# Six layer norms finished block by block inside the last products, the router likewise, and expert tokens split in the order of their columns

## The chip, the core and the metric

The kernel runs on one core of one Trainium2 chip. The metric is the device time of one execution in microseconds (us), from its first to its last instruction with what lies around them. TensorE (PE) multiplies a stationary operand, which a separate load instruction brings into the array, with a moving operand; VectorE (DVE), ScalarE (ACT) and GpSimd (POOL) do the rest, and SyncE (SP) issues nearly all DMAs. Before: 2105.73 us, the median of 3 runs (2105.18 to 2108.71).

## What is computed

A first network of two layers on 256 tokens of 1024 columns, each layer three steps with a layer norm behind each, and then a second block with a gated mixer and a mixture of 32 experts:

```python
for l in range(DEPTH):                      # DEPTH = 2
    x = _layernorm(ALPHA * x + 0.5 * _swiglu(x, ffn1_w_in[l], ffn1_w_out[l]), ln1_g[l], ln1_b[l])
    mix = _hybrid_mixer(x, l, ...)
    x = _layernorm(ALPHA * x + mix, ln2_g[l], ln2_b[l])
    x = _layernorm(ALPHA * x + 0.5 * _swiglu(x, ffn2_w_in[l], ffn2_w_out[l]), ln3_g[l], ln3_b[l])
...
h = modulate(rms_norm(x, norm_mix), shift1, scale1)
x = x + gate1[:, None, :] * mixed           # mixed from h
h2 = modulate(rms_norm(x, norm_ffn), shift2, scale2)
x = x + gate2[:, None, :] * hierarchical_moe(h2, ...)   # top 2 of 8 experts in the top group of 4
```

## The kernel before

The 256 tokens are two blocks of 128 rows (`tb` 0 and 1). Every fp32 matrix product is made of three with operands split into a rounded part and its remainder (`hi`, `lo` of weights; `xh`, `xl`, `hh`, `hl` of activations): `split` (L303) casts on ACT and subtracts on DVE. Weights come tile by tile: `wload` (L278) has a DMA of 512 KB on SP into one of 4 `raw` buffers, then a split into 5 `hi` and 5 `lo` buffers. `execute` (L257) walks the list of weight tiles and has the loads run two tiles ahead.

The kernel is written against a framework that puts each engine's instructions into an order of its own: by the order in which they are written, by what is ready in its model of time, and by priority (`high_priority(n)` moves instructions ahead by n; `keep_in_program_order` fixes one where it is written). Buffers are taken from pools (`big`: 14 tiles of 128x2048). Each engine then works strictly in its order.

**The end of each step.** `outp` (L440) makes the output product. For each of its `kt` weight tiles (22 after an FFN, 8 after a mixer) it issues, for both token blocks, six products of 512 columns (two column halves, three products each). The last four tiles are held: all their 24 products for block 0 come first, then `fn(0)`, then the 24 for block 1, then `fn(1)`. `fn` is the closure of `finisher` (L478): residual and statistics (L500, L501), mean and variance (L503), reciprocal root with a power on POOL (L313, L314), gain and bias (L508, L509). In `fn(1)` first block 0's x is turned by `to_T` (L519): eight PE transposes (L331) of 128x128 into PSUM, then `split` into `xhl`, the stationary or moving operand of the next step; at its end block 1's x likewise. In the last of the six norms (`mod=True`) `fn` also calls `modnorm` (L1256): squares on ACT, mean and power, then on DVE two passes with gain (L1275) and shift (L1277) held as rows for all partitions (`gain1`, two DMAs that copy a row to 128 partitions).

**The start of each step.** `tok` with `lead=True` (L349; mixer and second block) or `lead` in `ffn` (L545) collect its four weight tiles and then issue block 0's products (24, or 48 of half the columns) and block 1's. Tiles 1 and 2 (tile 1 in the second block) are split into `s2` buffers early (`SPARE`, `SPARE2`).

**The router.** `gated` (L1829) makes the same for the second block: `head` scales the router's weights and makes 16 small instructions for constant logits during the mixer; `fn(tb)` adds the gated result to x (L1859, L1860), squares (L1264), turns x (L1869), makes logits of 36 columns (L1873) and calls `tokens` (L1928): ACT writes rms-scaled tokens (L1933), DVE their remainder (L1935), both in a permuted order, column q*8+k to place k*128+q. `moe` (L2250) adds x to the output by eight products with the identity (L2257), `route` (L1938) is a chain of some 40 small DVE instructions to a one-hot table and places. `batch` (L2212) then builds selection matrices `P` (L2220) and gathers the tokens of four experts with PE (L2245): stationary 128 columns of the token tiles (tile name `raw`), moving `P`; 8 batches x 8 column groups x 4 products are 256. The experts' products are L2085 and L2122, the scatter L2141. `turn` (L2097) has the only stationary operand with a step between columns: L2107 reads every second column of `hs`, beside L2103, which reads contiguous `Pw`.

Of the kernel before, what the change touches and what calls it, by code (L numbers as in the profile page):

```python
# [18 lines left out]
NB = 2  # L19
# [12 lines left out]
PRIO = {'narrow': 300, 'rope2': 300}  # L32

SPARE, SPARE2 = (1, 2), (1,)

SUBY = (3, 9, 13)
TWO_PI = 2.0 * math.pi
# [69 lines left out]
class Net:  # L107
    def __init__(self, ctx, tc, I):
# [18 lines left out]
        self.side = None  # L127

# [149 lines left out]
    def wload(self, src, a, b, spare=False):  # L278
# [6 lines left out]
        if spare:  # L285
# [7 lines left out]
        self.split(hi[:, :n], lo[:, :n], raw[:, :n])  # L293
# [9 lines left out]
    def split(self, hi, lo, src):  # L303
        self.nc.scalar.copy(hi, src)  # L304
        self.nc.vector.tensor_tensor(lo, src, hi.bitcast(F32), op=ALU.subtract)  # L305
# [22 lines left out]
    def transposes(self, src, n=4):  # L328
        pt = self.bank([128, n, 128])
        for k in range(n):  # L330
            self.nc.tensor.transpose(pt[:, k, :], src[:, k * 128:(k + 1) * 128], self.ident)  # L331
# [3 lines left out]
    def mm_tok(self, ys, tb, ah, al, wh, wl, start, stop, parts=(0, 1)):  # L335
        mm = self.nc.tensor.matmul
        t = slice(tb * 128, tb * 128 + 128)
        for i in parts:
            for j, y in enumerate(ys):
                c = slice(j * 512, min(j * 512 + 512, wh.shape[1]))  # L340
# [8 lines left out]
    def tok(self, xT, w, c0, fn, n=512, lead=False, spare=SPARE):  # L349
# [10 lines left out]
        def tile(j):  # L360
            def run(wh, wl):
# [16 lines left out]
        for j in range(parts):  # L378
            self.W(w[:, kn * j:kn * j + kn, c0:c0 + n], kn, n, tile(j), lead and j in spare)
# [60 lines left out]
    def outp(self, aT, w, kt, fn, last=4, pre=None, order=None, join={}, pre_at=None, tail=None):  # L440
# [3 lines left out]
        def one(k, wt, tb, parts=(0, 1)):  # L444
            ah, al = aT(order[k])
            self.mm_tok(st["ys"][tb], tb, ah, al, wt[0][:, 0, :], wt[1][:, 0, :], k == 0, k == kt - 1, parts)

        def tile(k):
            def run(wh, wl):
# [12 lines left out]
                if k == kt - 1:  # L462
                    for tb in range(NB):
                        for part in ((0,), (1,)):
                            for i, wt in enumerate(st["w"]):
                                one(kt - last + i, wt, tb, part)
                        fn(tb, st["ys"][tb])
            return run

        for k in range(kt):  # L470
# [4 lines left out]
            self.W(w[:, order[k]:order[k] + 1, :], 1, D, tile(k))  # L475


    def finisher(self, S_, g, b, mod=False):  # L478
# [3 lines left out]
        def pre():  # L482
# [5 lines left out]
            if mod:  # L488
                st["m"] = self.modrows(0, 1, "gain1")
                st["h"] = self.t8([128, NB, D], F32, "h1")  # L490

        def fn(tb, ys):
            x = S_["x"][:, tb, :]
            src = st["h"] if mod else st["x"]
            if tb == NB - 1:
                self.to_T(S_, src, 0)
# [19 lines left out]
        return pre, fn  # L516


    def to_T(self, S_, x, tb):  # L519
# [3 lines left out]
        for j in range(2):  # L523
            pt = self.transposes(x[:, tb, j * 512:(j + 1) * 512])
            o = (slice(None), slice(4 * j, 4 * j + 4), slice(tb * 128, tb * 128 + 128))
            self.split(xh[o], xl[o], pt)
        if tb == NB - 1:
            S_["xT"] = (xh, xl)


    def ffn(self, S_, w_in, w_out, g, b, mod=False, first=False, side=None):
# [13 lines left out]
        def lead():  # L545
# [11 lines left out]
            def tile(j):  # L557
                def run(wh, wl):
# [9 lines left out]
                    for tb in range(NB):  # L568
                        ps = st["ps"][tb]
                        if not first:  # L570
                            for i in range(4):
                                one(i, tb)
                        sg = self.sc([128, 256], F32, "sg", True)
                        nc.scalar.activation(sg, ps[:, 0:256], AF.Silu)
# [13 lines left out]
            for j in range(4):  # L588
                c0 = (j // 2) * D_FF
                self.W(win[:, 4 * (j % 2):4 * (j % 2) + 4, c0:c0 + 256], 4, 256, tile(j), not first and j in SPARE)  # L590
# [25 lines left out]
        for f in range(1, KF // 2):  # L616
            pair(f)
            if f == 1 + first and side is not None:
                self.side = (side, 18, 4 * (KF // 2 - 2 - first) + KF - 4, 0)
        pre, fn = self.finisher(S_, g, b, mod)  # L620
        self.outp(lambda k: (H[k // 8][0][:, k % 8, :], H[k // 8][1][:, k % 8, :]), wout, KF, fn, pre=pre)
# [53 lines left out]
    def mixer(self, S_, l, L):  # L675
# [110 lines left out]
        pre, fn = self.finisher(S_, I["ln2_g"][l], I["ln2_b"][l])  # L786
        self.outp(lambda k: (L["m"][0][:, k, :], L["m"][1][:, k, :]), wo, KD, fn, pre=pre)
# [468 lines left out]
    def modnorm(self, x, G, out):  # L1256
        self.modnorm2(x, G, out, self.modnorm1(x))

    def modnorm1(self, x):
        nc = self.nc  # L1260
        ss = self.small.tile([128, 2], F32, name="ssm", tag="ssm")
        t = [self.sc([128, 512], F32, "mn") for _ in range(2)]
# [6 lines left out]

    def modnorm2(self, x, G, out, st):  # L1270
        nc = self.nc
        ss, t = st
        for n in range(2):
            c = slice(n * 512, n * 512 + 512)
            nc.vector.scalar_tensor_tensor(t[n], x[:, c], ss[:, 0:1], G[:, 1, c], op0=ALU.mult, op1=ALU.mult)  # L1275
            o, i0, i1 = out(n, t[n], G[:, 0, c])
            nc.vector.tensor_tensor(o, i0, i1, op=ALU.add)  # L1277

    def block2(self, S_, us):
# [42 lines left out]
        for it in BLOCK2.split():  # L1322
# [14 lines left out]
            else:  # L1337
# [4 lines left out]
        self.DO(lambda: (B.update(pj=True), B["head"]()))  # L1342
        wo = I["w_out_2"][0].rearrange("(k p) n -> p k n", p=128)
        pre, fn, B["head"] = self.gated(S_, B)
        self.outp(lambda k: [a[:, k % 4, :] for a in B["m", k // 4]], wo, KD, fn, pre=pre, order=(4, 5, 6, 7, 0, 1, 2, 3),
                  join={4: "gdn"}, pre_at=4, tail=lambda: us[1]["gu"]())
# [482 lines left out]
    def gated(self, S_, B):  # L1829
# [9 lines left out]
        def head():  # L1839

            t = self.hi_p.tile([128, 1024], F32, name="hi", tag="hi")
            wr, B["wr"] = (t[:, i * 288:i * 288 + 288].rearrange("p (k n) -> p k n", k=KD) for i in range(2))
            nc.sync.dma_start(wr[:, :, 0:4], I["w_group_2"][0].rearrange("(k p) n -> p k n", k=KD))
            nc.sync.dma_start(wr[:, :, 4:36], I["w_router_2"][0].rearrange("(k p) n -> p k n", k=KD))
            nc.vector.tensor_tensor(B["wr"], wr, self.modc[:, 32:40].rearrange("p (k o) -> p k o", o=1).to_broadcast([128, KD, 36]), op=ALU.mult)
            ps = self.bank([128, 36], pj=True)
            for k in range(KD):
                nc.tensor.matmul(ps, self.modc[:, 24 + k:25 + k].to_broadcast([128, 128]), wr[:, k, :], start=k == 0, stop=k == KD - 1)
            B["lc"] = self.route_p.tile([128, 36], F32, name="lc")
            nc.vector.tensor_tensor(B["lc"][:, 0:4], ps[:, 0:4], self.v2["b_group_2"], op=ALU.add)  # L1850
            nc.vector.tensor_tensor(B["lc"][:, 4:36], ps[:, 4:36], self.v2["b_router_2"], op=ALU.add)
            B["rs"], B["t"], B["lo"] = [], [], []

        def fn(tb, ys):
# [6 lines left out]
            if tb == 0:  # L1861
                B["pr"] = self.bank([128, 2, 36], pj=True)
            nrm = self.modnorm1(x)
            B["rs"].append(nrm[0][:, 0:1])
            hT = []
            for j in range(2):
                pt = self.bank([128, 4, 128], pj=True)
# [573 lines left out]
```

## Time and profile before

| | |
|---|---|
| median of 3 runs | 2105.73 us (2105.18 to 2108.71) |
| profiled execution, its time / its span | 2107.98 / 2106.2 us |
| PE busy | 2057.2 us, 98% |
| DVE, ACT, POOL busy | 70%, 52%, 4% |
| mean granted TensorE clock | 0.990 |
| DMA | 427.6 MB, mean 203 GB/s |

Busy is the time in which an engine executes, as a share of the span from first to last instruction. An idle time is put down to what released the engine, most often a semaphore of another engine's instruction. A line as L331 can be that of a helper that several callers use; the tile names tell them apart. Product ends are modelled, so 24 products that follow each other have a pace (start to start) that is shorter than the duration of one.

### The profile page before, as it was taken

How to read it: one execution, taken by the hardware profiler on the slowest of the kernel's cores; microseconds unless marked ns; L12 is line 12 of the kernel's file. 1: busy time of each engine (PE TensorE's matmuls, PEld its weight loads, DVE VectorE, ACT ScalarE, POOL GpSimd, SP SyncE). 2: the span in 40 equal slices, each digit the busy share in tenths (PEclk: the TensorE clock that was granted, in tenths of full speed). 3: DMA queues.
4: the chain of work that ended last, by engine and by line, in shares of the span. 5: the costliest groups of instructions: out<-in, count | busy, mean ns of one | idle time of the engine just before them, and what ended most of it. 6: DMA issues, size and time to landing. Idle time of an engine off the chain costs nothing.

```text
span 2106.2 us, 30863 instructions
## 1 busy us (share of the span) xinstructions
PE 2057.2 (98%) x11507; PEld 1650.7 (78%) x11507; DVE 1470.6 (70%) x2782; ACT 1105.4 (52%) x2026; POOL 75.3 (4%) x64
## 2 busy tenths in 40 slices
PE   8999999999999999999999999999998999899998
PEld 7887877888888888888877888888887878645543
DVE  6886688987878677875688896877666675533333
ACT  5654565777655544554466776754553554322222
POOL 0000000100000000000000110000000121001000
PEclk9999999999999999999999999999999989999999
DMA  7985544454659676876544355565674423799996
GB/s 229 304 261 175 166 133 135 129 162 141 192 193 303 190 256 197 273 242 205 162 123 142 109 161 169 151 224 167 188 235 137 136 63 116 265 364 357 357 374 235
DMA packets 278825, 427.60 MB, mean 203 GB/s; under 512 B 21806, under 2 KB 206352, under 8 KB 277648
## 3 DMA queue, kind: packets, MB, share of 16 engines
q1 hardware_dynamic: 278240, 422.44, 61.6%
q0 software_dynamic: 432, 3.15, 0.4%
q8 instruction: 92, 1.51, 0.3%
q14 instruction: 61, 0.50, 0.1%
HBM read 424.46 MB, written 1.07 MB: 202 GB/s over the span
## 4 chain that ended last, share of the span: by engine, by line
PE 86%; DVE 8%; ACT 2%; issue 1%; POOL 1%; DMA 0%; SPq 0%; ACTq 0%; POOLq 0%; DVEq 0%
PE ps L408 27%; PE ps L411 14%; PE ps L2085 6%; PE y L342 5%; PE y L343 5%; PE y L345 4%; PE ps L2122 3%; PE ps L342 3%; PE ps L345 3%; PE ps L343 3%; DVE lo L305 2%; PE ps L2245 2%; PE y L2141 1%; PE y L331 1%; PE ps L301 1%
## 5 line engine op out<-in xcount | busy, mean ns | idle before, releaser
L305 DVE TENSOR_TENSOR lo<-raw,hi 128x1024 fp32r<-128x1024 f32 (+1 forms) x556 | 660.2, 1196 | 250.5 <-ACT hi L304 175.0
L304 ACT CAST hi<-raw 128x1024 fp32r<-128x1024 f32 (+1 forms) x556 | 556.6, 1028 | 337.5 <-PE y L345 169.6
L408 PE MATMUL ps<-xhl,hi 128*128 128x512 f32 x2240 | 568.4, 395 | 0.8 <-DVE kc L181 0.8
L408 PEld LDWEIGHTS ps<-xhl,hi 128*128 128x128 f32 x2240 | 402.1, 189 | 76.2 <-issue 3.3
L411 PEld LDWEIGHTS ps<-xhl,lo 128*128 128x128 f32 x2240 | 306.1, 190 | 21.7
L411 PE MATMUL ps<-xhl,lo 128*128 128x256 f32 x2240 | 314.7, 283 | 0.0
L342 PE MATMUL y<-hi,hh 128*128 128x512 f32 x352 | 137.3, 390 | 0.0
L343 PE MATMUL y<-lo,hh 128*128 128x512 f32 x352 | 137.0, 389 | 0.0
L342 PE MATMUL ps<-hi,xhl 128*128 128x512 f32 (+1 forms) x304 | 121.8, 402 | 3.5 <-DVE ra L803 2.2
L2085 PE MATMUL ps<-wgu,hi 128*64 128x512 f32 x512 | 121.1, 594 | 0.0
L345 PE MATMUL ps<-hi,xhl 128*128 128x512 f32 (+1 forms) x304 | 118.7, 393 | 1.9 <-DVE xhl L305 1.9
L343 PE MATMUL ps<-lo,xhl 128*128 128x512 f32 (+1 forms) x304 | 120.1, 395 | 0.0
L179 ACT ACTIVATE ysum<-ps 128x256 f32<-128x256 f32 x168 | 64.3, 383 | 77.4 <-PE ps L411 73.4
L345 PE MATMUL y<-hi,hl 128*128 128x512 f32 x352 | 104.5, 389 | 0.0
L2085 PEld LDWEIGHTS ps<-wgu,hi 128*64 128x64 f32 x512 | 42.6, 137 | 68.2 <-issue 64.7
L181 DVE TENSOR_TENSOR ysum<-ysum,ps 128x256 f32<-128x256 f32 x168 | 69.3, 415 | 29.0 <-ACT ysum L179 28.7
L342 PEld LDWEIGHTS y<-hi,hh 128*128 128x128 f32 x352 | 66.1, 188 | 14.8 <-issue 1.2
L345 PEld LDWEIGHTS y<-hi,hl 128*128 128x128 f32 x352 | 66.1, 188 | 13.7
L343 PEld LDWEIGHTS y<-lo,hh 128*128 128x128 f32 x352 | 66.1, 188 | 13.5
L342 PEld LDWEIGHTS ps<-hi,xhl 128*128 128x128 f32 x304 | 58.2, 192 | 19.4 <-ACT qs L795 3.0
L179 ACT ACTIVATE sg<-ps 128x256 f32<-128x256 f32 x80 | 30.4, 380 | 80.5 <-PE ps L411 80.4
L345 PEld LDWEIGHTS ps<-hi,xhl 128*128 128x128 f32 x304 | 58.1, 191 | 15.8 <-DVE xhl L305 4.3
(604 smaller groups left out, 3192.8 us busy)
## 6 DMA issues: line engine op xcount, KB each, us to landing
raw<-in_w_mix_in_dram SPq DMA_DIRECT2D x184, 512.0 KB
raw<-in_ffn_w_in_dram SPq DMA_DIRECT2D x176, 512.0 KB
raw<-in_ffn_w_out_dram SPq DMA_DIRECT2D x88, 512.0 KB
wgu<-in_w_gate_dram SPq DMA_DIRECT2D x64, 512.0 KB
wgu<-in_w_up_dram SPq DMA_DIRECT2D x64, 512.0 KB
lo<-in_w_down_dram SPq DMA_DIRECT2D x54, 512.0 KB
wada<-in_w_ada_dram SPq DMA_DIRECT2D x96, 256.0 KB
raw<-in_w_branch_dram SPq DMA_DIRECT2D x48, 512.0 KB
```

The source lines that it names most:

```text
L179: self.nc.scalar.activation(out, pb, AF.Copy, scale=scale)
L181: self.nc.vector.tensor_tensor(out, out, pa, op=ALU.add)
L304: self.nc.scalar.copy(hi, src)
L305: self.nc.vector.tensor_tensor(lo, src, hi.bitcast(F32), op=ALU.subtract)
L342: mm(y, ah[:, t], wh[:, c], start=start, stop=False)
L343: mm(y, ah[:, t], wl[:, c], start=False, stop=False)
L345: mm(y, al[:, t], wh[:, c], start=False, stop=stop)
L408: mm(ps.rearrange("p (a b) -> p a b", a=2), h[:, k % 4, c], xh.both(k), start=k == 0, stop=False)
L411: mm(ps[:, 0:256], l[:, k % 4, c], xh[:, k, :], start=False, stop=k == KD - 1)
L2085: mm(gu[64 * e:64 * e + 64, c], u["x"](k)[:, 64 * e:64 * e + 64], w, start=k == 0 and i == 0, stop=k == KD - 1 and i == len(ws[0]) - 1)
L2122: mm = lambda *a, **kw: self.placed(pin, self.nc.tensor.matmul(*a, **kw))
L2245: nc.tensor.matmul(ps[:, j, :], B["t"][tb][i][:, 128 * k:128 * k + 128], P[:, tb, :], start=n == 0, stop=n == 3)
```

## The change

1. **Plain and modulated norms.** `outp` holds 6 tiles (8 before the second block) in place of 4 after FFNs and mixers of the first network; the first 2 (4) of them lie in `big` tiles. Block 1's products go by column halves. Before the last 6 (8) products of the second half, `mid` turns block 0 (fixed order). `fn` gets a priority of 300. Block 1 is turned by `late`, which the next step's lead calls between its products for block 0 and for block 1; in `ffn`'s lead both activations come behind both blocks' products, the first one fixed. The lead's fourth tile is split early too, and loads for early splits run up to four tiles ahead.
2. **The modulated norm.** `fn` only scales rows (half on ACT, half on DVE); gain and shift are applied after the turn, where columns lie on partitions: four instructions on ACT for the first half, four on DVE for the second, into a tile that is then split. The row copies go. `late` here also runs the constant logits of `head`, whose two loads are issued with the norm's.
3. **The router.** `outp` for the second block calls `mid` after 12 of the 16 steps of block 1: block 0's eight turns. `fn(1)` interleaves turns and logits; the split of block 0's tokens, and of block 1's, has a fixed place.
4. **Token order.** `tokens` writes rows unpermuted; `gather` reads every eighth column as its stationary operand, and the extra unit permutes when it copies from PSUM.

```diff
-SPARE, SPARE2 = (1, 2), (1,)
+SPARE, SPARE2 = {1: "s2", 2: "s2", 3: "big"}, {1: "s2", 2: "s2", 3: "own"}
+TAIL, TAIL_BIG, MID = (6, 8), (2, 4), (18, 24)
...
-                while nxt < len(ws) and len(loaded) <= ahead:
+                while nxt < len(ws) and len(loaded) <= (4 if ws[nxt][5] else ahead):
...
                 if lead:
                     if j == parts - 1:
                         for tb in range(NB):
+                            if tb == NB - 1:
+                                self.late()
                             for i, wt in enumerate(st["w"]):
                                 one(i, *wt, tb)
...
                     for tb in range(NB):
-                        for part in ((0,), (1,)):
-                            for i, wt in enumerate(st["w"]):
-                                one(kt - last + i, wt, tb, part)
-                        fn(tb, st["ys"][tb])
+                        halves = [(0,), (1,)] if mid is not None and tb == NB - 1 else [(0, 1)]
+                        for n, (c, part, i) in enumerate((c, p, i) for c in halves for p in (0, 1) for i in range(last)):
+                            if len(halves) > 1 and n == mid[0]:
+                                mid[1]()
+                            one(kt - last + i, st["w"][i], tb, (part,), c, len(halves) > 1 and last == 4 and n >= mid[0])
+                        with self.tc.high_priority(prio) if prio else ExitStack():
+                            fn(tb, st["ys"][tb])
...
             if mod:
-                h = st["h"][:, tb, :]
-                self.modnorm(st["x"][:, tb, :], st["m"], lambda n, t, s: (h[:, n * 512:n * 512 + 512], t, s))
+                x, h = st["x"][:, tb, :], st["h"][:, tb, :]
+                r = self.modnorm1(x, [h[:, 0:512], h[:, 512:1024]])[0][:, 0:1]
+                nc.scalar.activation(h[:, 0:512], x[:, 0:512], AF.Identity, scale=r)
+                nc.vector.tensor_scalar(h[:, 512:1024], x[:, 512:1024], r, None, op0=ALU.mult)
             if tb == NB - 1:
                 S_["x"] = st["x"]
-                self.to_T(S_, src, 1)
+                self.late, self.pin = late, True
+        def mid():
+            with self.tc.high_priority(PRIO["norm"]):
+                self.to_T(S_, st["h"] if mod else st["x"], 0, mod)
+        def late():
+            self.pin = False
+            if mod:
+                next(self.B["head"])
+            with self.tc.high_priority(PRIO["norm"]):
+                self.to_T(S_, st["h"] if mod else st["x"], 1, mod)
...
+            if mod:
+                y = self.sc([128, 4, 128], F32, "modx", True)
+                for k in range(4):
+                    shift, gain = (self.modc[:, i + 4 * j + k:i + 4 * j + k + 1] for i in (0, 8))
+                    if j:
+                        self.nc.vector.tensor_scalar(y[:, k, :], pt[:, k, :], gain, shift, op0=ALU.mult, op1=ALU.add)
+                    else:
+                        self.nc.scalar.activation(y[:, k, :], pt[:, k, :], AF.Identity, scale=gain, bias=shift)
+                pt = y
             self.split(xh[o], xl[o], pt)
...
-        to = lambda a: a.rearrange("p (k q) -> p q k", k=KD)
-        xv = x.rearrange("p (q k) -> p q k", k=KD)
-        nc.scalar.activation(to(th), xv, AF.Identity, scale=r)
+        nc.scalar.activation(th, x, AF.Identity, scale=r)
         B["t"].append((th, tl))
-        B["lo"].append(lambda: nc.vector.scalar_tensor_tensor(to(tl), xv, r, to(th).bitcast(F32), op0=ALU.mult, op1=ALU.subtract))
+        B["lo"].append(lambda: self.tc.keep_in_program_order(
+            nc.vector.scalar_tensor_tensor(tl, x, r, th.bitcast(F32), op0=ALU.mult, op1=ALU.subtract)))
...
-                    nc.tensor.matmul(ps[:, j, :], B["t"][tb][i][:, 128 * k:128 * k + 128], P[:, tb, :], start=n == 0, stop=n == 3)
+                    nc.tensor.matmul(ps[:, j, :], B["t"][tb][i][:, k:D:KD], P[:, tb, :], start=n == 0, stop=n == 3)
```

The calls of `outp` and the router's `fn` in the changed kernel:

```diff
-        self.outp(lambda k: (H[k // 8][0][:, k % 8, :], H[k // 8][1][:, k % 8, :]), wout, KF, fn, pre=pre)
+        self.outp(lambda k: (H[k // 8][0][:, k % 8, :], H[k // 8][1][:, k % 8, :]), wout, KF, fn, last=TAIL[mod], pre=pre,
+                  big=TAIL_BIG[mod], mid=(MID[mod], mid), prio=PRIO["norm"])
...
+            turned(1, 0)
+            logits(0, 0)
+            logits(0, 1)
+            turned(1, 1)
+            logits(1, 0)
+            logits(1, 1)
+            B["lo"][0]()
+            nrm = self.modnorm1(x)
```

## Rows read from the trace of the kernel before

**Rows 1.** The page's engines: busy us, share of the span, instructions.
```profile
PE 2057.2 (98%) x11507; PEld 1650.7 (78%) x11507; DVE 1470.6 (70%) x2782; ACT 1105.4 (52%) x2026; POOL 75.3 (4%) x64
```
**Rows 2.** Who waited, PE: line, releaser, us in total, times, longest.
```profile
PE y L331 <- DVE h L1277: 5.3, 2, 4.6
...
PE y L331 <- DVE x L509: 2.9, 5, 0.8
...
PE ps L1869 <- DVE x L1860: 2.7, 1, 2.7
PE ps L301 <- DVE xhl L305: 2.4, 6, 0.6
...
PE ps L345 <- DVE xhl L305: 1.9, 3, 1.2
...
PE ps L299 <- ACT xhl L304: 1.1, 3, 0.4
...
PE ps L342 <- ACT xhl L304: 0.7, 2, 0.3
```
**Rows 3.** Timeline of PE behind two norms: start, us, instruction [idle <-releaser].
```profile
200.38 1.04 PE L331 MATMUL y<-ctab,x 128*128 128x128 f32 x8
...
211.03 0.50 PE L345 MATMUL ps<-hi,xhl 128*128 128x512 f32 x1 [0.33 <-DVE xhl L305]
...
635.99 0.39 PE L301 MATMUL ps<-hi,xhl 128*128 128x256 f32 x1 [0.56 <-DVE xhl L305]
```
**Rows 4.** Timeline of DVE, first norm, block 0.
```profile
194.90 1.28 DVE L500 SCALAR_TENSOR_TENSOR x<-x,y 128x512 f32<-128x512 f32 x2 [1.88 <-PE y L345]
...
199.05 1.41 DVE L509 SCALAR_TENSOR_TENSOR x<-x,rs,lngb 128x512 f32<-128x512 f32 x2
```
**Rows 5.** Timeline of DVE, modulated norm, block 0: its first and last instruction.
```profile
1613.27 1.29 DVE L500 SCALAR_TENSOR_TENSOR x<-x,y 128x512 f32<-128x512 f32 x2 [2.90 <-PE y L345]
...
1622.76 1.29 DVE L1277 TENSOR_TENSOR h<-mn,gain 128x512 f32<-128x512 f32 x2
```
**Rows 6.** Stretch behind it: us, busy (instructions) of PE, PEld, DVE, ACT, POOL; clock; DMA.
```profile
1621.80:1632.04 10.24, 7.34 (x20) 5.53 (x21) 10.24 (x24) 2.67 (x7) 0.92 (x1) 0.50 0.21 54
```
**Rows 7.** Timeline of PE, router: logits of both blocks, first gather.
```profile
1819.84 1.98 PE L1873 MATMUL ps<-hi,xT 128*128 128x36 f32 x16 [0.29 <-ACT xT L1871]
...
1826.11 3.63 PE L1873 MATMUL ps<-hi,xT 128*128 128x36 f32 x16
...
1836.79 0.47 PE L2245 MATMUL ps<-P,raw 128*128 128x256 f32 x2 [0.90 <-DVE P L2220]
```
**Rows 8.** Timeline of DVE, router: the split of block 1's tokens.
```profile
1830.56 1.97 DVE L1935 SCALAR_TENSOR_TENSOR raw<-x,ssm,raw 128x1024 fp32r<-128x1024 f32 x1
```
**Rows 9.** Timeline of ACT: a contiguous cast, and the permuted tokens.
```profile
1617.58 1.05 ACT L304 CAST hi<-raw 128x1024 fp32r<-128x1024 f32 x1 [8.46 <-PE y L345]
...
1826.64 2.05 ACT L1933 ACTIVATE raw<-x,ssm 128x1024 fp32r<-128x1024 f32 x1
```
**Rows 10.** Stretches of the router and of the experts, columns as in rows 6.
```profile
1823.19:1833.43 10.24, 8.40 (x25) 5.97 (x26) 5.60 (x21) 3.94 (x6) 0.56 (x1) 0.50 0.84 340
...
1836.79:2096.00 259.21, 258.89 (x1278) 127.61 (x1280) 93.24 (x207) 57.67 (x136) 8.93 (x6) 1.00 0.90 344
```
**Rows 11.** Timeline of stationary loads (PEld): turns of `Pw`, of `hs`, the gather.
```profile
1994.86 0.20 PEld L2103 LDWEIGHTS y<-ctab,Pw 128*128 128x128 f32 x2 [0.81 <-issue]
1995.03 0.31 PEld L2107 LDWEIGHTS y<-ctab,hs 128*128 128x128 f32 x2
1995.26 1.96 PEld L2245 LDWEIGHTS ps<-P,raw 128*128 128x128 f32 x16
```
**Rows 12.** Lines L2245 and L2107 by themselves: min/median/max ns, first and last start us, forms.
```profile
L2245 PEld LDWEIGHTS ps<-P,raw x256: 186/188/201, 1836.8 to 2057.3; 128*128 128x128 f32 x128
L2245 PE MATMUL ps<-P,raw x256: 276/279/392, 1836.8 to 2057.4; 128*128 128x256 f32 x128
...
L2107 PEld LDWEIGHTS y<-ctab,hs x34: 195/200/220, 1857.7 to 2090.0; 128*128 128x128 f32 x32, 64*128 64x128 f32 x2
```

More of the change, by code (lines that the diff above doesn't have):

```diff
@@ L284, in wload @@
             self.nc.sync.dma_start(rv[:, :, c], s)
-        if spare:
+        if spare == "big":
+            t = self.big.tile([128, 2048], F32R, name="wtail", tag="b8")
+            hi, lo = (t[:, i * 1024:i * 1024 + 1024] for i in range(2))
+            self.split(hi, lo, raw)
+            return (hi.rearrange("p (a b) -> p a b", a=a), lo.rearrange("p (a b) -> p a b", a=a))
+        if spare == "s2":
             hi, lo = ([self.s2.tile([128, 512], F32R, name=i, tag="sc") for _ in range(2)] for i in ("hi", "lo"))
@@ L378, in tok @@
         for j in range(parts):
-            self.W(w[:, kn * j:kn * j + kn, c0:c0 + n], kn, n, tile(j), lead and j in spare)
+            self.W(w[:, kn * j:kn * j + kn, c0:c0 + n], kn, n, tile(j), lead and spare.get(j))
     def fm(self, xT, w, c0, fn, wide=True):
@@ L474, in outp @@
                 self.JOIN(join[k])
-            self.W(w[:, order[k]:order[k] + 1, :], 1, D, tile(k))
+            self.W(w[:, order[k]:order[k] + 1, :], 1, D, tile(k), "big" if 0 <= k - (kt - last) < big else None)
     def finisher(self, S_, g, b, mod=False):
@@ L568, in run @@
                     for tb in range(NB):
-                        ps = st["ps"][tb]
                         if not first:
+                            if tb == NB - 1:
+                                self.late()
                             for i in range(4):
                                 one(i, tb)
+                    for tb in range(NB):
+                        ps = st["ps"][tb]
                         sg = self.sc([128, 256], F32, "sg", True)
-                        nc.scalar.activation(sg, ps[:, 0:256], AF.Silu)
+                        a = nc.scalar.activation(sg, ps[:, 0:256], AF.Silu)
+                        if tb == 0 and not first:
+                            self.tc.keep_in_program_order(a)
                         nc.vector.scalar_tensor_tensor(sg, sg, 0.5, ps[:, 256:512], op0=ALU.mult, op1=ALU.mult)
@@ L589, in lead @@
                 c0 = (j // 2) * D_FF
-                self.W(win[:, 4 * (j % 2):4 * (j % 2) + 4, c0:c0 + 256], 4, 256, tile(j), not first and j in SPARE)
+                self.W(win[:, 4 * (j % 2):4 * (j % 2) + 4, c0:c0 + 256], 4, 256, tile(j), not first and SPARE.get(j))
         def pair(f):
@@ L1253, in modrows, with modnorm1 @@
         return t
-    def modnorm(self, x, G, out):
-        self.modnorm2(x, G, out, self.modnorm1(x))
-    def modnorm1(self, x):
+    def modnorm1(self, x, t=None):
         nc = self.nc
         ss = self.small.tile([128, 2], F32, name="ssm", tag="ssm")
-        t = [self.sc([128, 512], F32, "mn") for _ in range(2)]
+        t = t or [self.sc([128, 512], F32, "mn") for _ in range(2)]
         for n in range(2):
@@ L1837, in pre, with turned, logits, mid @@
                 nc.sync.dma_start(B["SG"][:, i, :], self.mod[24 + 8 * i:32 + 8 * i, :].rearrange("(o f) p -> o (f p)", o=1).rearrange("o (p k) -> (o p) k", k=KD))
[L1839 to L1852, printed above, removed]
+        hT = {}
+        def turned(tb, j, pin=False):
+            pt = self.bank([128, 4, 128], pj=True)
+            for k in range(4):
+                t = nc.tensor.transpose(pt[:, k, :], S_["x"][:, tb, (4 * j + k) * 128:(4 * j + k + 1) * 128], self.ident)
+                if pin:
+                    self.tc.keep_in_program_order(t)
+            hT[tb, j] = self.sc([128, 4, 128], F32, "xT2")
+            nc.scalar.copy(hT[tb, j], pt)
+        def logits(tb, j):
+            for k in range(4 * j, 4 * j + 4):
+                nc.tensor.matmul(B["pr"][:, tb, :], hT[tb, j][:, k % 4, :], B["wr"][:, k, :], start=k == 0, stop=k == KD - 1)
+        def mid():
+            B["pr"] = self.bank([128, 2, 36], pj=True)
+            for j in range(2):
+                turned(0, j, True)
         def fn(tb, ys):
```

103 lines of the change are left out of this document (55 added, 48 removed).

## The prediction

> **What bounds the kernel now.** I read the page's engine table first: TensorE (PE) is busy 98% of the span, DVE 70%, so what moves the end is PE's idle time, its clock, or the length of its own instructions [rows 1]. Next the list of who waited for whom, for PE alone: the largest entries are turns (transposes, L331) and first products behind a layer norm, and the turn at the router [rows 2]. Then the stretches themselves: PE at the end of a plain norm [rows 3], DVE there [rows 4], DVE at the last norm, the modulated one [rows 5], the clock behind it [rows 6], the router on PE and DVE and ACT's passes [rows 7 to 9], and clock and load of router and experts [rows 10]. From the router on PE is busy 258.9 of 259.2 us, with DMA at 0.90 beside it: an experts' stage in which anything that makes a PE instruction longer lengthens the program. Last, single loads of stationary operands, because the change alters how one family of 256 of them reads SBUF [rows 11, 12].
>
> **Part A, the five plain norms.** Before, block 0's turns follow all of block 1's products, and PE waits at four places: block 1's x before its turns (2.9 us in all five), ACT's first half xhl (1.1 and 0.7), DVE's xhl (2.4 at L301; 1.9 at L345, of which 1.2 belongs to the modulated norm) [rows 2]. That is 7.8 us. The wait that follows block 1's turns, 0.33 us before a mixer and 0.56 before an FFN [rows 3], stays, since `late` still puts turns directly ahead of the products that need them: 2 x 0.33 + 3 x 0.56 = 2.3. So 5.5 us can go. Is each cover there? A product takes 0.228 us (24 of them fill about 194.90 to 200.38 [rows 3, 4]). With six held tiles PE runs 30 of block 1's 36 products, 6.8 us, before block 0's turns; that block's norm needs 194.90 to 200.46, 5.6 us [rows 4]. Six products, 1.4 us, then cover the split. Block 1's first columns end 5 us earlier than its last, so half of its x and statistics are done by then and its norm ends some 4.7 us behind the last product, under block 0's 5.5 us of next products. What is late next is a weight split standing in DVE's order ahead of the norm: 1.2 us each. I take -5.0, with bounds +1 and -7.8. The held tiles and early lead loads cost nothing beside this: the same DMAs and splits come earlier on SP, ACT and DVE, whose slack is there; without it a split of about 2.3 us (ACT then DVE) would show. Two broadcast DMAs (`gain1`) leave SP's queue; POOL keeps one power per norm.
>
> **Part B, the modulated norm.** [...] After: block 0's chain is 1613.27 to 1624.05, 10.8 us, less the two gain and shift passes on DVE (2.6) plus one scaling (0.7): about 8.5 [rows 5]; PE has 40 of 48 products before the turns, 9.1 us. Block 1's chain ends about 8 us after the last product, and PE fills 5.5 us with products and 2.0 with the 16 instructions of `head` (their like take 1.98 [rows 7]), so about 0.5 us of wait. Then the turned block must be scaled and shifted (four small instructions on ACT, four on DVE) before it is split; PE waits about 1.7 us there. That leaves 2.2 to 3 us of wait with little dense work between, so the clock may fall again, for less work than before. I take -5.0: 4 from waits, 1 from the clock; bounds -1 and -9.
>
> **Part C, the router.** Block 0's logits start at 1819.84 and the experts' first product at 1836.79; inside lie the wait of 2.7 for x behind a DVE pass that took its place, block 1's logits at the low clock (3.63 us against 1.98) and DVE's routing chain from 1829.74, with a split of tokens of 1.97 inside [rows 2, 7, 8, 10]. After: block 0's eight turns (1 us) move ahead of the last products; then turns and two blocks of logits, 5 us at the full level or about 7 if it falls again; routing without its split, 5.1; the split of block 1's tokens, now pinned behind the slot tables, about 1.4 (two contiguous halves of such a DVE pass take 1.41 [rows 4]), and the first experts' products wait for it. Together 12.5 to 14.5 instead of 18.3 from the last product on, less the moved 1 us: 3 to 5. The eight identity products of L2257 lie beside routing; if the clock is low they can end last. I take -5.0, the upper end, as ACT's pass over the tokens halves as well; bounds -1 and -8.
>
> **Part D, the gather's stationary operand.** `tokens` now writes rows as they stand, and `gather` reads every eighth column: 256 loads with a step of 32 bytes [rows 12]. No strided load of such a kind stands in the trace, so bounds from the nearest rows. Low end, no cost: the gather's loads follow each other every (1.96 - 0.19) / 15 = 0.118 us [rows 11, 12], and the one strided load there is, `turn`'s at L2107 with a step of two elements, still follows its neighbour after 0.31 - 0.20 = 0.11 us [rows 11, 12]. High end, a doubling: that same pair of loads takes 0.31 us where the contiguous pair of L2103 beside it takes 0.20 [rows 11], and ACT writing one element per 512 bytes takes 2.05 us for what it does contiguously in 1.05 [rows 9]. The logits of 36 columns, where the loads alone set the pace, take 1.98 us for 16, (1.98 - 0.28) / 15 = 0.113 each [rows 7, 12]; doubled, 0.22. 256 x (0.22 - 0.118) = 26 us, all on PE's path, as PE never idles there [rows 10]; I take +25 for a first load now and then hidden under the products before it. I choose the high end because two engines in the trace lose half their rate as soon as neighbours in the pattern are not neighbours in memory. A gain has no reason here: contiguous is already the best pattern.
>
> [...]
>
> **The sum.** -5 - 5 - 5 + 25 = +10 us. The profiled execution took 2107.98 us (span 2106.2), 2.25 above the median 2105.73 of the runs; it would become 2118, the median 2116. Own range of this case: 2108 to 2123 from gains of 8 to 23.
>
> **Rivals.** First, on the other side: strided loads keep the pace of 0.118, part D is nothing, and 2105.7 - 15 = 2091 (2082 to 2098). For it: `turn`'s loads at step two just meet that pace. Against: the halved rates. It decides at 15 / 256 = 0.06 us per load: below a spacing of 0.18 the change is a gain. Second, between: loads get slower but only by about half, to 0.16; 256 x 0.045 = 11.5, so 2102. Third: the gather as forecast, but in-order queues eat the gains: pinned turns of block 0 wait because a weight split stands before the norm on DVE, 1.2 us at each of five norms and twice at the modulated one, and PE's clock falls at both late places; gains of 3 are left, 2128. Fourth: the compiled order hardly changes, since priorities only advise it; norms gain nothing, about 2125.
>
> **How the numbers follow.** Forecast 0.44, first rival 0.38, second 0.08, third 0.07, fourth 0.03. A measurement of this kernel tells some 0.2% (4 us) from no change. Faster: 0.37 of the first and 0.04 of the second, 0.41. Within: 0.01 + 0.04 + 0.04 from the forecast's low end, 0.09. Slower: 0.50. The range takes in both likely cases, from 2085 to 2122; about 0.08 is left out below and as much above.
>
> **What would show it.** The pace of the 256 gather products: 16 in about 3.5 us instead of 2. PE's waits at L331 and the xhl splits: about 2.5 us left of 7.8, one per norm and after block 1's turns only. One wait of at most 2 us at the modulated norm's late turns, and the length of its low clock. From the router's last product to the first gather, 12 to 14 us instead of 18. Wrong it would be by a gather that keeps its pace, above all; next by DVE taking splits first.

## The result, and the profile after

The changed kernel takes 2131.92 us (median of 4 runs, 2128.00 to 2133.76) where the kernel before takes 2107.22 beside it: a ratio of 1.0112, 95% interval 1.0092 to 1.0132, 25 us slower. I had forecast 2116. Its profiled execution took 2133.76 us with a span of 2132.0; against the one of before (2107.98 and 2106.2) that is 25.8 us more, and the rest of this part says where they lie.

The page's engines after, as in [rows 1]: PE is still busy 98%, now for 2088.2 us instead of 2057.2, with the same 11507 instructions. So the instructions got longer; no new idle time explains the loss: busy time grew by 31.0 us, the span by 25.8.

```profile
PE 2088.2 (98%) x11507; PEld 1684.9 (79%) x11507; DVE 1468.4 (69%) x2787; ACT 1111.4 (52%) x2037; POOL 76.3 (4%) x64
```

I cut both spans at five instructions that can be found in every kernel's PE timeline: the first product of 512 columns (L408, after: L427), the last such product ahead of the modulated norm, the product behind the 0.46 us wait for ACT's `sqkv` (L342, after: L351), the last product that waits for `gzo` (L1558, after: L1599), and the first gather (L2245, after: L2313). In brackets: time of the stretch in which PE was granted half its clock (0.50 in [rows 6]), below called the low clock, and PE's idle time, in the last row up to PE's last product.

| stretch, us | before | after | difference |
|---|---|---|---|
| start | 26.45 | 24.99 | -1.46 |
| two layers with the five plain norms | 1531.24 (0; 13.7) | 1527.33 (3.4; 11.2) | -3.91 |
| modulated norm, block 2's first projections | 110.27 (10.2; 7.1) | 111.54 (13.7; 4.3) | +1.27 |
| rest of block 2 | 143.24 (20.5; 9.8) | 144.55 (23.9; 11.3) | +1.31 |
| router | 25.58 (10.2; 4.4) | 22.55 (6.8; 2.6) | -3.03 |
| experts, to the end | 269.41 (3.1; 0.4) | 301.01 (4.3; 0.3) | +31.60 |

The gather's line by itself, after (min/median/max ns, first and last start, forms). The rows of before are the first two of [rows 12]: 188 ns a load, 279 a product.

```profile
L2313 PEld LDWEIGHTS ps<-P,raw x256: 312/337/343, 1830.9 to 2082.8; 128*128 128x128 f32 x128
L2313 PE MATMUL ps<-P,raw x256: 398/402/518, 1831.0 to 2082.9; 128*128 128x256 f32 x128
```

Successive products start 0.240 us apart (median over the line's own starts) instead of 0.118, and 256 x 0.122 = 31.2 us: nearly the whole of the last stretch's 31.6.

Who waited after, PE, columns as in [rows 2]. Of the five `L331 <- DVE x` waits of before one is left (1.2), the xhl splits at L313 (before: L301) are as long in sum but three instead of six, and the modulated norm has two new waits: a weight split `lo` (2.4) and ACT's xhl (1.4 of the 1.7).

```profile
PE ps L351 <- DVE lo L317: 2.4, 1, 2.4
PE ps L313 <- DVE xhl L317: 2.4, 3, 1.3
...
PE ps L351 <- ACT xhl L316: 1.7, 2, 1.4
...
PE ps L1885 <- DVE x L1907: 1.5, 1, 1.5
...
PE y L343 <- DVE x L532: 1.2, 1, 1.2
...
PE ps L351 <- DVE xhl L317: 1.1, 2, 0.7
...
PE ps L311 <- ACT xhl L316: 0.2, 1, 0.2
```

PE at the modulated norm after: the lead products stop 2.41 us for `lo`, the 16 instructions of the router's constant (L1935) take 3.46 us, block 1's eight turns 1.95, and the next product waits 1.39.

```profile
1621.93 0.50 PE L351 MATMUL ps<-lo,xhl 128*128 128x512 f32 x1 [2.41 <-DVE lo L317]
...
1623.76 3.46 PE L1935 MATMUL ps<-wr,mod 128*128 128x36 f32 x16
1627.03 1.95 PE L343 MATMUL y<-ctab,h 128*128 128x128 f32 x8
1630.37 0.80 PE L351 MATMUL ps<-hi,xhl 128*128 128x512 f32 x1 [1.39 <-ACT xhl L316]
```

What DVE did meanwhile: it took block 1's norm (L531, L532) first, then the weight split that PE waited for, then the split of the next weights, and block 1's h last.

```profile
1618.02 1.40 DVE L531 SCALAR_TENSOR_TENSOR x<-x,mv,lngb 128x512 f32<-128x512 f32 x2
1619.34 1.40 DVE L532 SCALAR_TENSOR_TENSOR x<-x,rs,lngb 128x512 f32<-128x512 f32 x2
1620.66 1.22 DVE L317 TENSOR_TENSOR lo<-raw,hi 128x1024 fp32r<-128x1024 f32 x1
...
1622.13 1.21 DVE L317 TENSOR_TENSOR lo<-raw,hi 128x1024 fp32r<-128x1024 f32 x1
1623.79 0.48 DVE L538 TENSOR_SCALAR h<-x,ssm 128x512 f32<-128x512 f32 x1 [0.44 <-POOL ssm L1317]
```

And the stretches at the low clock after, at the modulated norm and at the router, columns as in [rows 6]:

```profile
1622.51:1636.17 13.66, 12.27 (x42) 10.23 (x41) 6.53 (x12) 4.98 (x9) 1.24 (x1) 0.50 0.53 168
...
1820.49:1827.31 6.82, 6.82 (x25) 5.27 (x25) 1.82 (x14) 3.04 (x7) 0.55 (x1) 0.50 1.00 396
```

### The profile page after: what moved, and what is told of

Read it like the earlier page. It is cut to its first block, busy times and chain, and to the rows that moved or that the text cites. A ratio compares the mean times of both kernels' runs of the same rounds, so it can differ in the third digit from the quotient of the medians.

```text
span 2132.0 us, 30878 instructions
## 1 busy us (share of the span) xinstructions
PE 2088.2 (98%) x11507; PEld 1684.9 (79%) x11507; DVE 1468.4 (69%) x2787; ACT 1111.4 (52%) x2037; POOL 76.3 (4%) x64
## 4 chain that ended last, share of the span: by engine, by line
PE 88%; DVE 7%; ACT 2%; issue 1%; POOL 1%; DMA 0%; SPq 0%; ACTq 0%; POOLq 0%; DVEq 0%
PE ps L427 27%; PE y L351 14%; PE ps L430 14%; PE ps L351 8%; PE ps L2150 6%; PE ps L2187 3%; PE ps L2313 3%; DVE lo L317 2%; PE y L2206 1%; PE y L343 1%; PE ps L313 1%; PE ps L312 1%; PE ps L311 1%; DVE cv L1010 1%; PE y L1117 1%
## 5 line engine op out<-in xcount | busy, mean ns | idle before, releaser
L317 DVE TENSOR_TENSOR lo<-raw,hi 128x1024 fp32r<-128x1024 f32 (+2 forms) x538 | 637.0, 1192 | 221.2 <-ACT hi L316 142.5
L316 ACT CAST hi<-raw 128x1024 fp32r<-128x1024 f32 (+2 forms) x538 | 536.9, 1026 | 261.8 <-PE y L351 83.3
L427 PE MATMUL ps<-xhl,hi 128*128 128x512 f32 x2240 | 568.4, 395 | 0.8 <-DVE kc L185 0.8
L427 PEld LDWEIGHTS ps<-xhl,hi 128*128 128x128 f32 x2240 | 402.1, 189 | 76.2 <-issue 3.3
L351 PE MATMUL ps<-hi,xhl 128*128 128x512 f32 (+1 forms) x592 | 192.0, 398 | 5.5 <-DVE ra L856 2.2
L351 PEld LDWEIGHTS ps<-hi,xhl 128*128 128x128 f32 x592 | 112.0, 192 | 34.5 <-ACT qs L848 3.0
L351 PE MATMUL y<-lo,hh 128*128 128x512 f32 x312 | 121.5, 389 | 0.0
L351 PE MATMUL y<-hi,hh 128*128 128x512 f32 x312 | 121.4, 389 | 0.0
L351 PE MATMUL ps<-lo,xhl 128*128 128x512 f32 (+1 forms) x296 | 117.3, 396 | 2.4 <-DVE lo L317 2.4
L351 PE MATMUL y<-hi,hl 128*128 128x512 f32 x312 | 92.9, 389 | 0.0
L351 PEld LDWEIGHTS ps<-lo,xhl 128*128 128x128 f32 x296 | 57.1, 193 | 14.5 <-DVE lo L317 2.8
L351 PEld LDWEIGHTS y<-hi,hl 128*128 128x128 f32 x312 | 58.6, 188 | 12.3
L351 PEld LDWEIGHTS y<-lo,hh 128*128 128x128 f32 x312 | 58.6, 188 | 12.0
L351 PEld LDWEIGHTS y<-hi,hh 128*128 128x128 f32 x312 | 58.6, 188 | 12.0
L316 ACT CAST yh<-yg 128x512 fp32r<-128x512 f32 (+1 forms) x34 | 21.0, 617 | 88.0 <-DVE yg L2195 88.0
```

Source lines behind the costliest of these rows:

```text
L317: return self.nc.vector.tensor_tensor(lo, src, hi.bitcast(F32), op=ALU.subtract)
L351: mm = lambda *a, **kw: self.placed(pin, self.nc.tensor.matmul(*a, **kw))
L427: mm(ps.rearrange("p (a b) -> p a b", a=2), h[:, k % 4, c], xh.both(k), start=k == 0, stop=False)
```

## Experiments

Ratios are against the kernel before on the same chip; 0.1% is 2.1 us.

**Part D alone, on the kernel before.** Tokens in the columns' order, gather at a step of eight:

```
-  nc.scalar.activation(to(th), xv, AF.Identity, scale=r)
+  nc.scalar.activation(th, x, AF.Identity, scale=r)
...
-  nc.tensor.matmul(ps[:, j, :], B["t"][tb][i][:, 128 * k:128 * k + 128], P[:, tb, :], ...)
+  nc.tensor.matmul(ps[:, j, :], B["t"][tb][i][:, k:D:KD], P[:, tb, :], ...)
```

> The kernel before with part D alone: tokens kept in the columns' order, the gather's stationary operand read at a step of eight elements (32 bytes). Theory (the strided weight loads set the pace, and they alone cost what the gather lost): the gather's product goes from 0.118 to 0.24 us here too, 256 x 0.122 = 31 us, less about 1 us for the tokens' two passes without their permuted write, so 29 to 32 us over the kernel before. Rival (the gather of the whole change was also slowed by what lies around it, and D alone costs the 25 us that I forecast or less): 20 to 26 us over.

Measured: 2138.08 us, ratio 1.0141 (1.0125 to 1.0156), +30 us (26 to 33); the last stretch, cut as above, is 30.5 us longer than before. The gather's line in this kernel, columns as above:

```profile
L2245 PEld LDWEIGHTS ps<-P,raw x256: 312/337/343, 1836.6 to 2087.6; 128*128 128x128 f32 x128
```

The loads are those of the changed kernel to the nanosecond. The theory holds; the rival (25 us or less) falls.

**The change with D undone.** The same three places turned back in the changed kernel.

> The changed kernel with part D alone undone: tokens permuted when they are split, the gather's operand side by side again. Theory (D is the whole of the gather's 31.6 us, and the norms and the router keep the 5.8 us by which the first gather came earlier): about 31 us under the changed kernel, 4 to 7 us under the kernel before. Rival (what the norms gained is given back behind the first gather, by transfers or the clock): within 2 us of the kernel before.

Measured: 2103.81 us, 0.9984 (0.9974 to 0.9993): 28 us under the changed kernel, 3.4 under the kernel before. A little less than the 31 and the 4 to 7 I gave. PE's timeline at the first gather shows where some 2 us of it went: DVE's permuted passes over the tokens (L2002, 2.00 us each, where the changed kernel's take 1.28) now end last.

```profile
1830.71 0.18 PE L2072 MATMUL y<-onehot,bmask 128*128 128x32 bf16 x1 [1.02 <-DVE onehot L2069]
...
1834.05 2.36 PE L2313 MATMUL ps<-P,raw 128*128 128x256 f32 x10 [1.21 <-DVE raw L2002]
```

**How far apart may the elements stand?** The kernel before, its tokens kept in groups of S = 2 or 4 columns, so that the gather steps over 8 or 16 bytes:

```
-  to = lambda a: a.rearrange("p (k q) -> p q k", k=KD)
+  to = lambda a: a.rearrange("p (b q r) -> p b q r", b=KD // S, r=S)
...
-  B["t"][tb][i][:, 128 * k:128 * k + 128]
+  B["t"][tb][i][:, k // S * 128 * S + k % S:(k // S + 1) * 128 * S:S]
```

> The kernel before with its tokens kept in pairs of columns, so that the gather's stationary operand has a step of two elements (8 bytes); the tokens' split is four passes instead of one. [...] Rival (the price grows with the distance): 0.118 + 0.122/7 = 0.135 us a product, 4 to 5 us over. Rival (any step costs all): 0.24 us, 30 us over.

> The kernel before with its tokens kept in fours, so that the gather's operand has a step of four elements (16 bytes); the split is two passes. [...] Rival (the price grows with the distance): 0.118 + 0.122 x 3/7 = 0.17 us, 13 us over. [...]

Measured, one run each: 2107.65 and 2132.82 us, beside 2107.16 for the kernel before. The loads, first at 8 bytes, then at 16:

```profile
L2247 PEld LDWEIGHTS ps<-P,raw x256: 193/196/208, 1835.0 to 2056.8; 128*128 128x128 f32 x128
```

```profile
L2247 PEld LDWEIGHTS ps<-P,raw x256: 307/329/332, 1832.9 to 2081.9; 128*128 128x128 f32 x128
```

The loads take 188, 196, 329 and 337 ns at 4, 8, 16 and 32 bytes, with products 0.118, 0.120, 0.233 and 0.240 us apart. So nearly the whole price of the gather falls between 8 and 16 bytes: neither a price by distance (0.135 at 8, 0.17 at 16) nor one for any step.

**A layout that keeps both.** Tokens in the columns' order as in the change, but the experts' rows in pairs (row d = 256 b + 2 p + r), so the gather steps over 8 bytes:

```
-  I[nm][0, e].rearrange("(p k) n -> p k n", k=KD)[:, 4 * j:4 * j + 4, :]
+  I[nm][0, e].rearrange("(b p r) n -> p b r n", b=4, r=2)[:, 2 * j:2 * j + 2, :, :]
...
-  B["t"][tb][i][:, k:D:KD]
+  B["t"][tb][i][:, k // 2 * 256 + k % 2:(k // 2 + 1) * 256:2]
```

> The changed kernel, its tokens in the columns' order as they are, but the experts' rows laid out in pairs: the gather's stationary operand has a step of two elements (8 bytes) instead of eight, and the experts' gate and up weights are loaded in pieces of 2 KB instead of 4 KB. Theory: the gather keeps 0.118 to 0.12 us a product, and the tokens' passes stay short, so the waits of 1.0 and 1.2 us that the kernel with D undone showed at the first gather are gone too; with the 5.8 us that the changed kernel gained ahead of it, 4 to 8 us under the kernel before. Rival (transfers of half the piece are slower, where the experts' stage already has its DMA engines at 0.90): the products wait for weights, 5 us or more over the kernel before.

Measured: 2101.13 us, 0.9973 (0.9964 to 0.9982), 5.7 us under the kernel before, inside the 4 to 8 of the theory. Loads take 193 ns; pieces of 2 KB instead of 4 cost little that shows: in the kernel before with this layout alone (below) the last stretch takes 269.94 us, beside 269.41 without it. Of the two waits that the kernel with D undone had at the first gather, the one of 1.02 us is gone and the one of 1.21 for the tokens is 0.48.

```profile
L2317 PEld LDWEIGHTS ps<-P,raw x256: 192/193/209, 1824.4 to 2047.6; 128*128 128x128 f32 x128
```

**The same layout on the kernel before**, with nothing else of the change.

> The kernel before with its tokens in the columns' order and the experts' rows in pairs, and nothing else of the change. Theory (a load at a step of 8 bytes keeps its pace, pieces of 2 KB cost nothing, and the token passes lose their permuted writes: DVE's 1.97 us of block 1's tokens between the logits and the first gather becomes 1.2): 0.5 to 2 us under the kernel before. Rival (the experts' stage is longer by the 1.5 to 3 us by which the kernel of pairs took longer from its first gather to its end): 0.5 to 2 us over it.

Measured: 2105.17 us, 0.9988 (0.9979 to 0.9997), 2.5 under. The tokens' order by itself shortens the router from 25.58 to 23.96 us in the profiles; it is a gain, though a small one (0.6 to 4.4 us by the interval), once the loads don't pay for it.

**Each other part undone**, in the kernel of pairs: the plain norms (four held tiles, no `mid` and `late`), the modulated norm (rows of gain and shift, no `mid` and `late`, the constant back in block 2), the router (both blocks turned in `fn`). In short, in this order:

```
-  TAIL, TAIL_BIG, MID = (6, 8), (2, 4), (18, 24)
+  TAIL, TAIL_BIG, MID = (4, 8), (0, 4), (18, 24)
...
+  TAIL, TAIL_BIG, MID = (6, 4), (2, 0), (18, 24)
+  self.modnorm(st["x"][:, tb, :], st["m"], lambda n, t, s: (h[:, n * 512:n * 512 + 512], t, s))
...
-  tail=lambda: us[1]["gu"](), mid=(12, mid))
+  tail=lambda: us[1]["gu"]())
```

> The kernel of pairs with the five plain norms as in the kernel before (four held tiles, block 0's turns behind all products of the norm's input, block 1's turns at the norm, two lead splits aside); the modulated norm and the router stay changed. My forecast of part A: 5 us over the kernel of pairs. What the rows of the changed kernel say (3.8 us over the five norms, one of which lost 1.1): 3 to 5 us over it. If the parts add up (5.8 us of the kernel of pairs, 1.8 by undoing the modulated norm, 2.3 by undoing the router), only 1 to 2.5 us are left for this one.

> The kernel of pairs with the modulated norm as in the kernel before (gain and shift as rows, block 0 turned behind all products, the router's constant in block 2's second half); plain norms and router stay changed. My forecast of part B: 5 us over the kernel of pairs. What the rows of the changed kernel say (0 to 1.3 us lost there: 2.7 us less of waits, against the constant's products of 3.5 us moved into the low clock, and 3.4 us more of low clock): 0 to 2 us under it.

> The kernel of pairs with the router as in the kernel before (both blocks turned behind all products, block by block, the tokens' split inside the routing), but with the short token passes kept. My forecast of part C: 5 us over the kernel of pairs. What the rows of the changed kernel say (some 3 us gained from block 2's last product to the first gather): 2 to 4 us over it.

Measured, beside the kernel of pairs at 0.9973 (all intervals are about 0.0009 either way, so a difference of two is known to some 2.7 us):

| undone | us | ratio | worth of the part |
|---|---|---|---|
| plain norms (A) | 2106.42 | 0.9993 | 4.2 |
| modulated norm (B) | 2103.44 | 0.9984 | 2.3 |
| router (C) | 2103.42 | 0.9982 | 1.9 |

With A undone the waits are those of [rows 2] again, five times x and six times xhl:

```profile
PE y L343 <- DVE x L534: 2.9, 5, 0.8
...
PE ps L313 <- DVE xhl L317: 2.3, 6, 0.6
```

The stretches of the profiles, cut as above (low clock; idle):

| kernel | plain norms | modulated norm | rest of block 2 | router | experts |
|---|---|---|---|---|---|
| pairs | 1525.93 (0; 11.3) | 107.83 (3.4; 4.7) | 142.95 (20.5; 11.1) | 22.38 (6.8; 2.4) | 272.28 |
| A undone | 1531.37 (0; 13.5) | 110.05 (10.2; 4.3) | 142.99 (20.5; 11.1) | 22.40 (6.8; 2.4) | 272.23 |
| B undone | 1527.58 (3.4; 11.4) | 110.25 (6.8; 8.0) | 143.62 (20.5; 10.8) | 20.87 (3.4; 2.5) | 272.24 |
| C undone | 1527.84 (3.4; 11.5) | 111.59 (13.7; 4.3) | 139.92 (13.7; 11.4) | 23.10 (6.8; 2.8) | 272.35 |
| pairs alone | 1531.39 (0; 13.7) | 110.26 (10.2; 7.2) | 143.27 (20.5; 10.0) | 23.96 (10.2; 2.4) | 269.94 |

Part A agrees with the 5 us that I forecast. For B and C the intervals just reach or miss the 5 us, and they take in 0 as well: by the times alone neither is shown to gain anything. What I had read for B from the changed kernel's rows, a loss of 0 to 2 us, did not come either. The modulated norm's column points to the reason for B: three kernels with the same instructions there take 107.83, 110.05 and 111.59 us with 3.4, 10.2 and 13.7 us of low clock, while B undone takes 110.25 with 3.3 to 3.7 us more of idle time. For C the profiles say no more: undone, the router is 0.7 us longer, but the rest of block 2 is 3.0 shorter, with 6.8 us less at the low clock. The parts' worths and the 2.5 us of the pairs sum to 10.9, not 5.7; the four intervals together allow an excess of about as much (some 5.4 us), so it may be noise. One loss does stand in the last column: 2.3 to 2.4 us behind the first gather in the first four kernels, which have the changed kernel's pinned token split, against the pairs alone. Of it 0.9 are in the first sixteen gather products, where PE waits for block 1's tokens. The rest of it I have not traced.

**The router's constant elsewhere.** Behind block 1's turns (the two statements in `late` swapped), and back in block 2:

> The kernel of pairs with one more edit: at the modulated norm the eight products of the router's constant stand behind the turns of block 1, not ahead of them. [...] Rival (that stretch ends with a chain of DVE and ACT, or the products only move the low clock): within 1 us of it.

> The kernel of pairs with the router's constant (eight products of 36 columns) back in block 2's second half, where the kernel before has it. [...] Rival (the low clock behind the norm's waits sets the stretch, and it varies from one execution to the next by more than that): no difference that five rounds can tell, within 2 us.

Measured: 2100.87 us, 0.9960 (0.9946 to 0.9974), and 2100.12 us, 0.9959 (0.9945 to 0.9972). Both intervals overlap that of the pairs, so these times can't tell the three places apart. The timelines can say what moved. With the constant behind the turns:

```profile
1625.76 1.97 PE L343 MATMUL y<-ctab,h 128*128 128x128 f32 x8 [1.19 <-ACT h L537]
1627.52 3.47 PE L1938 MATMUL ps<-wr,mod 128*128 128x36 f32 x16
1630.79 0.77 PE L351 MATMUL ps<-hi,xhl 128*128 128x512 f32 x1
```

The wait for the split is gone, but one for h took its place (1.19), and the modulated norm's stretch is 110.13 us at 10.2 of low clock, no better than A undone with the constant ahead (110.05 at the same). In block 2 the constant leaves 108.84 at 10.2 of low clock, 1.2 less, and block 2 is longer. In the kernel of pairs, whose clock stayed up until 1626.60, the same 16 instructions and turns take half the time:

```profile
1622.11 1.87 PE L1938 MATMUL ps<-wr,mod 128*128 128x36 f32 x16
1623.81 1.07 PE L343 MATMUL y<-ctab,h 128*128 128x128 f32 x8
1626.68 0.79 PE L351 MATMUL ps<-hi,xhl 128*128 128x512 f32 x1 [1.81 <-ACT xhl L316]
```

## Why the prediction was wrong, step by step

The sign was right and the sum was -15 + 25; measured in the profiles it is -5.8 ahead of the first gather and +31.6 behind it. So the changed kernel's profile lies 15.8 us above the forecast of +10: 6.6 of them in part D, 6.3 in B, 2.0 in C, 1.1 in A and 1.3 in block 2, less 1.5 of the start. Two steps failed, then: the price of a strided load was set too low, and the gains of the norms and the router were counted as waits removed, at 15 us, where the waits and the low clock that came in their place left 5.8, or 4.4 without the start, which the change does not touch. The range had no room for either, as it kept D at 25 and let the gains vary from 8 to 23.

- **Part D, the term that carried the sum, was mis-sized: 25 forecast, 30 to 31 measured.** The cause is the forecast one: the loads take 337 ns instead of 188, in D alone too, and the changed kernel's products follow 0.240 us apart instead of 0.118. The size came from doubling the pace of the logits' loads (0.113 to 0.22, rounded down: 0.226 would have given 28 us); the real pace is 0.240. And I took 1 us off for loads hidden under products, where none was: 256 x 0.122 = 31.2. The bound was drawn too tightly as well: 26 was a doubling, no upper end. One of the two halved rates that I argued from was a comparison of unlike passes: ACT's 1.05 us was a cast, and its pass over the tokens takes 1.15 without the permuted write.
- **The first rival (strided loads keep the pace) and the second (0.16 us)** are refuted by D alone, 30 us. What I had set against each other, a pace kept as at `turn`'s step of two [rows 11] and the doubling, both hold for the gather, the one at 8 bytes (0.120) and the other at 16 and 32 (0.233 and 0.240). I read the step of two as half an argument for the step of eight; it said nothing about it.
- **Part A: -5.0 forecast; -3.9 in the changed kernel's profile, -5.3 in that of the pairs, 4.2 by undoing it.** Right within its bounds, but not by the waits alone, and so partly by luck. Of 7.8 us of waits 5.5 were to go and 2.6 went: x 1.2 and xhl 2.4, 1.1, 0.3 and 0.2 are left. PE's idle time in the stretch fell by 2.5 and 2.4 us; the rest of the gain, 1.4 and 2.9, is time in which PE counts as busy, and why that is shorter was not traced. Where the changed kernel fell short, weight splits, which I had named as "what is late next", stood ahead of block 1's norm: its x of layer 0's second norm came 1.20 us late, and the clock then fell for 3.4 us (632.65 to 636.06). The kernel of pairs has the same wait (1.2) without the fall.

```profile
630.42 1.31 PE L343 MATMUL y<-ctab,x 128*128 128x128 f32 x8 [1.20 <-DVE x L532]
...
632.82 0.58 PE L313 MATMUL ps<-hi,xhl 128*128 128x256 f32 x1 [0.56 <-DVE xhl L317]
```

- **Part B: -5.0 forecast, +1.3 in the changed kernel, 2.3 us of gain by undoing it, known to 2.7. Three terms failed.** (1) "Block 1's chain ends about 8 us after the last product": it took 10.1 (the last product's end at 1614.45 to h at 1624.51), since a weight split, block 0's own splits and small products of L1253 stand in DVE's order, and POOL's power took 1.46 us instead of 0.55 (below). The waits left are 2.4 + 1.4 = 3.8, not 2.2 to 3; of the 5.3 + 1.2 = 6.5 before [rows 2] that is 2.7 less, where the forecast has 4. (2) The constant's 16 instructions cost 3.46 us on the path, not 2.0 of filler. (3) I gave the clock a gain of 1 us, which no run shows; the stretch at the low clock grew from 10.24 us [rows 6] to 13.66, and PE's work in it from 7.34 to 12.27. If half of that work is lost time (an estimate from the granted 0.50), 2.5 us more are lost. That the clock might fall again was in the text; that its fall, with the constant's products moved here (1.87 us at a clock of 1.00 in the kernel of pairs), outweighs 2.8 us less of idle time was not. A slip in block 0's chain did no harm: 10.8 - 2.6 + 0.7 is 8.9, not 8.5, and its turns still did not wait.
- **Part C: -5.0 forecast, -3.0 measured; of these 1.6 come from the tokens' order alone** (router 25.58 to 23.96 us with the pairs alone), and undoing the turns costs 1.9 us of time, known to 2.7. I had taken the upper end of 3 to 5. The terms that I named add to 11.5 to 13.5 us, not the 12.5 to 14.5 that I wrote; from the last product's end (1816.78) to the first gather it took 14.2. What ends last is what I had set beside the routing: the eight identity products run until 1829.59, behind logits of block 1 at the low clock (3.46 us), and PE then waits only 0.20 us for DVE's table.

```profile
1818.26 0.63 PE L1885 MATMUL ps<-ctab,x 128*128 128x128 f32 x4 [1.47 <-DVE x L1907]
...
1821.28 3.46 PE L1893 MATMUL ps<-hi,xT 128*128 128x36 f32 x16
1824.55 5.04 PE L2325 MATMUL y<-x,ctab 128*128 128x512 f32 x8
1829.79 0.18 PE L2070 MATMUL y<-onehot,bmask 128*128 128x32 bf16 x1 [0.20 <-DVE onehot L2067]
```

- **The third rival (weight splits ahead of the norm, a clock that falls at both late places, 2128)** was closest to what happened, though I gave it 0.07. Its splits stood at one plain norm and at the modulated one instead of at all. Its number is near in part by luck: it has the gather at 25 and the gains at 3, where 31.6 and 5.8 were measured.
- **Not in the forecast:** block 2's stretch is 1.3 us longer (3.4 us more of low clock; waits for `pr` of 0.2, 0.8 and 0.2 us that were not there), and the start 1.5 us shorter, which the change does not touch: it was between 24.8 and 26.5 in all thirteen profiles.

## What to carry to other kernels

Before a stationary operand is read with a step, look at the distance in bytes: for the gather here, 8 bytes left the pace of its products at 0.120 us instead of 0.118, 16 and 32 doubled it (0.233 and 0.240), and in a stage where PE idles 0.4 us of 269 every nanosecond of the load's pace counts (31.2 us of the 31.6 lost here); a pair-wise layout of the other operand (here the weights' rows) kept the step at two elements, 193 ns a load. A gain counted in waits must be followed through the clock: here, behind a wait of 2.4 us that was left, PE ran 13.7 us at 0.50 of its clock instead of 10.2 before, and the modulated norm's stretch was 1.3 us longer with 2.8 less of idle time. And before a chain on an in-order engine is priced by its own instructions, count what else that engine has queued between them (block 1's chain at the modulated norm took 10.1 us, not 8).

## What the runs showed of the hardware

**The price of the gather's load is a step, not a slope:** 188, 196, 329, 337 ns at 4, 8, 16 and 32 bytes between elements of four bytes. For another kind of load 8 bytes were not free in the kernel before: `turn`'s loads of `hs` at that step take 200 ns [rows 12], those of `Pw`, side by side, 141. What sets the two kinds apart was not tried.

```profile
L2103 PEld LDWEIGHTS y<-ctab,Pw x32: 137/141/144, 1857.5 to 2089.8; 128*128 128x128 f32 x32
```

**POOL's power took longer behind a DVE split.** It has one column, and takes 0.55 us at block 0's norm, where DVE ran nothing beside it, and 1.46 at block 1's, where a DVE weight split (1622.13 to 1623.34, both inputs in SBUF) had begun 0.16 us before it; it ends 0.4 us after the split. That held back h by 0.9 us.

```profile
1609.71 0.55 POOL L1317 TENSOR_TENSOR ssm<-ssm,mhalf 128x1 f32<-128x1 f32 x1 [3.26 <-DVE ssm L1316]
...
1622.29 1.46 POOL L1317 TENSOR_TENSOR ssm<-ssm,mhalf 128x1 f32<-128x1 f32 x1 [3.13 <-DVE ssm L1316]
```

No run changed this alone, and why POOL takes longer there is not shown. The thirteen profiles hold 52 such powers of `ssm`. All 7 that began behind a DVE split of that kind took 1.46 us. The other 45 took 0.55 or 0.56, among them 13 that began behind a DVE instruction with only one input in SBUF, as this one, whose y lies in PSUM:

```profile
1814.02 0.68 DVE L1906 TENSOR_TENSOR gt<-gates,y 128x512 f32<-128x512 f32 x1
1814.18 0.56 POOL L1317 TENSOR_TENSOR ssm<-ssm,mhalf 128x1 f32<-128x1 f32 x1 [6.63 <-DVE ssm L1316]
```

**The same instructions behind the same wait met different clocks.** After a wait of 2.41 or 2.42 us for the same split, the profiles show 13.7 us at the low level (changed, D undone, C undone), 10.2 (A undone) and 3.4 (pairs); the stretch then takes 111.6, 110.1 and 107.8 us. Differences of 4 us between single executions of this kernel are therefore no evidence for an edit; what sets the length of these falls stays open.
